# Splitting a kernel's weights by DMA: a cast on the way in, a negative, and an adding transfer

## The chip, the cores and the metric

The kernel runs on one core of a Trainium2 chip. The core has a matrix engine (TensorE, PE in the profile), a vector engine (VectorE, DVE), a scalar engine (ScalarE, ACT), a general engine (GpSimd, POOL) and a queue engine (SyncE, SP) that issues most transfers. Sixteen DMA engines, shared by all queues, move data between DRAM and the on-chip memory. The metric is the device time of one execution in microseconds, with the median of several runs; lower is better.

## The reference

One inference step of a two-layer recurrent decoder, in float32, for a prompt of 512 tokens and 8 single-token samples that share the weights (520 columns in all, width 1024). Cut to what matters here:

```
h  -> u = rmsnorm(h) @ w_in                     # layer 0: 1024 -> 5648
      a_out = RG-LRU(conv(a_x)) * silu(a_gate)
      b_out = groupnorm(SSD(conv(x, B, C), dt) * silu(z)) * w
h += concat(a_out, b_out) @ w_out               # 2048 -> 1024
h += sigmoid(h @ w_gate0) * (p0 @ w_proj0)      # 1024 -> 1024, 256 -> 1024

h  -> q, f, v, g = split(rmsnorm(h) @ w_in1)    # layer 1: 1024 -> 8192
      o = HGRN2(q, f, v) with 16 heads of 128
h += (rmsnorm_head(o) * silu(g)) @ w_out1       # 2048 -> 1024
h += sigmoid(h @ w_gate1) * (p1 @ w_proj1)
y  = rmsnorm(h)
```

The results are `y`, the recurrent states and the convolution buffers. Nearly all of the arithmetic is in the dense products with the weights, some 70 MB of float32.

## The kernel before

**Products.** Features lie on partitions, tokens along the free axis. Each dense product is made from float32r parts, a format of TensorE with fewer bits than float32: a weight tile w is split into `hi`, which is w cast to float32r, and `lo`, which is w − hi, and the activations are split likewise into xh and xl. A tile of 128 output features then takes, for each block of 128 input features, the products hi·xh, hi·xl and lo·xh, each over two halves of 260 columns (`project_both`, lines 682 to 701). A *unit* of weights is 128 × 1024 numbers, 512 KB; a full tile of outputs uses one unit in 8 × 6 = 48 matrix products. Two pairs of PSUM banks (`mmps`, line 560) take the outputs in turn, and ACT and DVE empty them.

**Weights.** `section` (line 609) cuts the matrices into units and puts neighbours into groups of one or two. `load_group` (line 619) loads a group of up to 1 MB from SP's queue into one of two raw buffers. `split_unit` (line 627) makes the parts: `hi` by a copy that casts, on ACT or DVE, whichever the plan finds free, and `lo` by a subtraction on DVE (POOL in two places at the start). Each part has two buffers, so a cast waits for the products of two units before. The sections come in the order in which they are used: `ax` (the RG-LRU input), the embedding's `proj0`, then `xbc` (12 units), `z`, `ag`, `z1`, `out0a`, `out0b`, `pg0`, `proj1`, and for layer 1 per pair of heads `f`, `v`, `q`, `g` with two units each, the output projection `o3`, `o5`, `o7`, `o8` with four units each, and `pg1`, the last gate.

**Order.** The program doesn't run in the order in which it is written. Every instruction is recorded with a place (`prio`) in the stream of dense products, which moves by 0.668 us for each block of six products (line 699). `side` shifts places earlier or later: loads by `LOAD_AHEAD` = 11.54 us, splits by `SPLIT_AHEAD` = 1.67 us. `Plan.order` (line 348) then lets an estimated clock run: an engine that comes free takes, of the instructions whose operands are there by that estimate, the one with the earliest place; instructions that the dense stream waits for are moved 38.78 us ahead. For a transfer it counts 1.0 us of POOL or 0.46 us of SP, 0.65 us until it starts, its bytes over 360 GB/s on one bus, and 1.0 us until it has landed (lines 466 to 472). The result is a fixed order for each engine; on the chip, semaphores make each instruction wait for its operands, and what is behind a waiting instruction on its engine waits with it.

**Around the dense stream.** In layer 0, ACT, DVE and POOL do the convolutions, the RG-LRU recurrence and the SSD scan. POOL computes the logarithm for `dt` in a row of small steps (`log1p_of`, line 920, called for `dt_project`, line 1168), prepares the sample columns and masks the decay matrices. In layer 1 each pair of heads has a chain of decay, products within chunks (A), key transposes (kt), states (kv) and outputs (o), whose matrix products PE takes between the dense ones, and POOL only takes a power of a few numbers per head.

**The last gate.** `layer1_end` (line 1973) goes over the tokens in two halves, each with all 8 units of `pg1`. Units 0 and 1 use the ordinary buffers; units 2 to 7 go to tiles of their own (`keep_acy`, `keep_z`, `keep_bx`) and stay for the second half. `pl1`, the embedding term of 2 MB, is loaded with one transfer 20 us ahead.

Nearly every instruction is issued at line 510, so the profile's groups are told apart by the names of tiles: `wraw` is a raw buffer, `whi` and `wlo` are the parts; a name such as `q` or `o` on PE is the output of that product.

Of the kernel before, what the change touches and what calls it, by code (L numbers as in the profile page):

```python
# [42 lines left out]
# how far ahead of a unit its weights are split and loaded, in us of the main stream  # L43
SPLIT_AHEAD, LOAD_AHEAD = 1.67, 11.54
# how far ahead of the main stream goes what it waits for, in us
MARGIN = 38.78
# an engine waits for an instruction that is more urgent by URGENT us, up to this part of the time of the one at hand
# [32 lines left out]
def _mm(n, a, k):  # L80
    out, m = k["out"] if "out" in k else a[0], k["lhsT"].shape[-1]
    if m < 128 and out.off >= 32 * ROW:
        # beside the one before it, in other columns of the array
        return 65 if k["rhs"].dtype == F32R else 125
    return max(n, 256) if k["rhs"].dtype == F32R else 4 * max(n, m)
# [17 lines left out]
class Buf:  # L103
    """A tile that is allocated when its first instruction is issued."""
# [7 lines left out]
class View:  # L112
    """A view of a Buf; offset and strides are in elements, a partition is ROW apart."""
# [86 lines left out]
class Op:  # L200
    """One instruction, in a form for each engine that may take it, or a few matrix products that stay together."""
# [8 lines left out]
class Plan:  # L210
    """Instructions are collected first and then put in an order: with an estimate of what each of them costs, an
    engine that comes free takes the instruction of the earliest place in the program whose operands are there."""
# [6 lines left out]
    # -- collecting --  # L219
# [23 lines left out]
    def side(self, start=0.0, rate=0.0, pinned=False):  # L243
        """Instructions whose place is moved, by a start and by their own time so far; pinned: for good."""
# [5 lines left out]
    @contextmanager  # L250
    def together(self, *views):
        """Instructions that wait until all of some operands are written."""
        self.gate = self.barrier([o for v in views for box, o, w in v.buf.acc if w and _meet(box, v.box())])
        yield
        self.gate = None

    @contextmanager
    def block(self, main=False):
        """Matrix products that stay together."""
# [66 lines left out]
    # -- ordering --  # L326
    def hold_banks(self):
        """A PSUM bank is taken only when what its readers wait for otherwise is already on its way."""
# [7 lines left out]
    def urgency(self):  # L336
        """What an instruction of the main stream waits for is put ahead of it."""
# [10 lines left out]
    def order(self):  # L348
# [44 lines left out]
        def pick(e, t):  # L393
            """The instruction for engine e at time t, or when there may be one."""
# [7 lines left out]
            while av:  # L402
# [13 lines left out]
                if func and table not in IN_SET[func]:  # L416
                    # another table: first what the loaded one can do, for a while
# [14 lines left out]
            if got:  # L432
                heapq.heappush(av, got)
                hold = {"dve": HOLD_DVE, "act": HOLD_ACT, "pool": HOLD_POOL}.get(e)
                if hold:
                    # rather wait a little for one that is more urgent than be in its way
# [8 lines left out]
        while left:  # L445
# [27 lines left out]
            else:  # L473
                if e == "pe":
                    # the clock is halved after a window with too few columns
# [17 lines left out]
    # -- issuing --  # L493
# [27 lines left out]
# the place of the side work: its start after the instructions it follows, and its pace  # L521
# [9 lines left out]
def hybrid_decode_step_kernel(ctx: ExitStack, tc: tile.TileContext, I, O, mode="both"):  # L531
# [31 lines left out]
    def grab(name):  # L563
        """One of four PSUM banks for the side work; it is given back by its last reader."""
# [26 lines left out]
    def copy(out, in_):  # L591
        """A copy on either engine."""
        plans[-1].record(("act", "copy", (out, in_), {}), ("dve", "tensor_copy", (out, in_), {}))

    def scaled(out, in_, s):
        """in_ times a column, on either engine."""
# [10 lines left out]
    groups, units, sec = [], [], {}  # L607

    def section(name, ap, k0, kk, c0, ncols, uc, per=2):
        sec[name] = len(units)  # L610
        for c in range(c0, c0 + ncols, per * uc):
            w = min(per * uc, c0 + ncols - c)
            groups.append((ap, k0, kk, c, w))
            for s in range(0, w, uc):
                units.append((len(groups) - 1, s, uc, kk))
# [3 lines left out]
    def load_group(g):  # L619
        ap, k0, kk, c, w = groups[g]  # L620
        r = new("wp", [128, 2048], "raw", f"wraw{g}", 2)
        v = r[:, :kk * w].rearrange("p (k c) -> p k c", k=kk)
        with side(*((plans[-1].shift, 0.0, True) if plans[-1].pinned else (-LOAD_AHEAD,))):
            sp.dma_start(out=v, in_=ap[k0 * 128:(k0 + kk) * 128, c:c + w].rearrange("(k p) c -> p k c", p=128))
        raw_of[g] = v

    def split_unit(u, hi=None, lo=None, eng=dve):
        g, s, uc, kk = units[u]
        if g not in raw_of:
            load_group(g)  # L630
        v = raw_of[g][:, :, s:s + uc]
        if hi is None:
            hi = new("wp", [128, 1024], "whi", f"whi{u}", 2, F32R)
            lo = new("wp", [128, 1024], "wlo", f"wlo{u}", 2, F32R)
        hv = hi[:, :kk * uc].rearrange("p (k c) -> p k c", k=kk)
        lv = lo[:, :kk * uc].rearrange("p (k c) -> p k c", k=kk)
        with side(*((plans[-1].shift, 0.0, True) if plans[-1].pinned else (-SPLIT_AHEAD,))):
            copy(hv, v)
            tt(lv, v, hv.bitcast(F32), SUB, eng)
# [5 lines left out]
    section("ax", w_in0, 0, 8, 0, 256, 128, 1)  # L645
    section("ax2", w_in0, 0, 8, 256, 768, 128)
    section("proj0", I["ple_proj"][0], 0, 2, 0, 512, 256, 1)
# [1456 lines left out]
```

## Time and profile before

| | |
|---|---|
| Median of 3 runs | 1074.88 us (1073.48 to 1077.2) |
| Profiled execution, first to last instruction | 1075.0 us |
| Mean granted clock of TensorE | 0.991 |
| Read from DRAM, written to DRAM | 111.71 MB, 25.44 MB |
| Weight loads of 1 MB on SP's queue | 32 + 15 + 8 + 8 + 8 + 1 |

The profile gives no other time for the profiled execution than its span, which is the time from its first to its last instruction. All views below are of this one execution. A group of instructions is shown by line, engine, operation, output and inputs with shapes and count, then the total busy time and the mean in ns of one, then the idle time of the engine just before them with what ended it. In a view of stretches each row has a stretch, its length, and the busy time and instruction count of each engine in it. The chain that ended last is followed back from the last instruction, each step to what released it.

### The profile page before, as it was taken

What the parts mean: (1) busy time and instruction counts of PE and PEld (TensorE: products, weight loads), DVE (VectorE), ACT (ScalarE), POOL (GpSimd) and SP (SyncE); (2) the same over time, 40 slices, a digit from 0 to 9 for tenths busy, and PEclk for the clock granted to TensorE, in tenths of its full rate; (3) what the DMA queues carried; (4) which work ended last, traced back from release to release, by engine and by line L of the source; (5) the groups of instructions that cost most, each with busy time, mean ns of one, the idle gap of its engine ahead of it and who ended that gap; (6) DMA issues with size and microseconds to landing.
All of it is one profiled execution on the core that took longest, in us unless ns stands there. A gap on an engine that the chain in (4) does not pass through costs nothing.

```text
span 1075.0 us, 21235 instructions
## 1 busy us (share of the span) xinstructions
PE 1044.0 (97%) x8595; PEld 1023.0 (95%) x8595; DVE 778.2 (72%) x1521; ACT 509.1 (47%) x1196; POOL 144.6 (13%) x247
## 2 busy tenths in 40 slices
PE   9899989999999999999999999999999999999995
PEld 8899988899999999999999999999999999999995
DVE  6879988999997546774858576675765757667753
ACT  6476648636464212353445545333463344642453
POOL 3755475200000000100000000000000000000000
PEclk9899999999999999999999999999999999999998
DMA  8603226444686233563433433253342433335311
GB/s 275 244 21 99 80 51 206 147 142 140 200 249 210 79 115 131 162 208 88 135 108 115 128 102 111 90 155 91 115 124 87 143 98 112 97 89 199 119 40 44
DMA packets 130466, 138.43 MB, mean 129 GB/s; under 512 B 13704, under 2 KB 111128, under 8 KB 130344
## 3 DMA queue, kind: packets, MB, share of 16 engines
q1 hardware_dynamic: 130136, 136.93, 41.0%
q8 instruction: 69, 1.13, 0.4%
q14 instruction: 37, 0.30, 0.1%
q0 software_dynamic: 224, 0.06, 0.0%
HBM read 111.71 MB, written 25.44 MB: 128 GB/s over the span
## 4 chain that ended last, share of the span: by engine, by line
PE 84%; POOL 5%; DVE 4%; DMA 3%; ACT 2%; issue 1%; POOLq 0%; ACTq 0%; DVEq 0%
PE o L510 11%; PE g L510 10%; PE f L510 9%; PE v L510 9%; PE q L510 9%; PE pg L510 7%; PE ag L510 4%; PE ob L510 4%; PE z L510 4%; PE oa L510 3%; PE ax L510 3%; PE xbc L510 1%; POOL csm L510 1%; PE A L510 1%; PE kv L510 1%
## 5 line engine op out<-in xcount | busy, mean ns | idle before, releaser
L510 DVE TENSOR_TENSOR wlo<-wraw,whi 128x1024 fp32r<-128x1024 f32 (+1 forms) x143 | 173.4, 1213 | 3.2 <-ACT whi L510 1.8
L510 ACT CAST whi<-wraw 128x1024 fp32r<-128x1024 f32 (+1 forms) x63 | 65.2, 1036 | 126.3 <-PE q L510 41.2
L510 POOL TENSOR_TENSOR at__1873<-at__1873,nhalf 128x4 f32<-128x4 f32 (+1 forms) x24 | 20.8, 866 | 501.1 <-DVE at__1873 L510 501.1
L510 DVE CAST whi<-wraw 128x1024 fp32r<-128x1024 f32 x80 | 55.3, 692 | 36.7 <-PE v L510 11.9
L510 PE MATMUL g<-xh,whi 128*128 128x260 f32 x256 | 55.8, 299 | 0.0
L510 PE MATMUL q<-xh,whi 128*128 128x260 f32 x256 | 53.2, 289 | 0.0
L510 PE MATMUL o<-oh,whi 128*128 128x260 f32 x256 | 52.6, 286 | 0.0
L510 PE MATMUL v<-xh,whi 128*128 128x260 f32 x256 | 52.1, 285 | 0.0
L510 PE MATMUL v<-xh,wlo 128*128 128x260 f32 x256 | 51.5, 283 | 0.0
L510 PE MATMUL g<-xl,whi 128*128 128x260 f32 x256 | 51.5, 283 | 0.0
L510 PE MATMUL o<-oh,wlo 128*128 128x260 f32 x256 | 51.5, 283 | 0.0
L510 PE MATMUL g<-xh,wlo 128*128 128x260 f32 x256 | 51.5, 283 | 0.0
L510 PE MATMUL o<-ol,whi 128*128 128x260 f32 x256 | 51.4, 282 | 0.0
L510 PE MATMUL q<-xl,whi 128*128 128x260 f32 x256 | 51.4, 282 | 0.0
L510 PE MATMUL v<-xl,whi 128*128 128x260 f32 x256 | 51.4, 282 | 0.0
L510 PE MATMUL q<-xh,wlo 128*128 128x260 f32 x256 | 51.4, 282 | 0.0
L510 PE MATMUL f<-xh,whi 128*128 128x260 f32 x240 | 50.6, 292 | 0.0
L510 PE MATMUL f<-xl,whi 128*128 128x260 f32 x240 | 48.2, 282 | 0.0
L510 PE MATMUL f<-xh,wlo 128*128 128x260 f32 x240 | 48.2, 282 | 0.0
L510 DVE SCALAR_TENSOR_TENSOR l1a<-q,lbt,l1a 128x260 f32<-128x260 f32 (+1 forms) x32 | 14.0, 479 | 44.1 <-PE q L510 44.0
L510 DVE SCALAR_TENSOR_TENSOR l1c<-l1d,l1c 128x128 f32<-128x128 f32 x128 | 40.9, 345 | 0.6 <-ACT l1c L510 0.6
L510 PEld LDWEIGHTS o<-oh,whi 128*128 128x128 f32 x256 | 39.3, 189 | 0.9 <-issue 0.8
(507 smaller groups left out, 3362.2 us busy)
## 6 DMA issues: line engine op xcount, KB each, us to landing
wraw<-in_c_w_in_dram SPq DMA_DIRECT2D x32, 1024.0 KB
wraw<-in_ab_w_in_dram SPq DMA_DIRECT2D x15, 1024.0 KB
wraw<-in_ab_w_out_dram SPq DMA_DIRECT2D x8, 1024.0 KB
wraw<-in_ple_gate_dram SPq DMA_DIRECT2D x8, 1024.0 KB
l1c<-in_state_c_dram SPq DMA_DIRECT2D x16, 512.0 KB
out_dram<-l1c SPq DMA_DIRECT2D x16, 512.0 KB
wraw<-in_c_w_out_dram SPq DMA_DIRECT2D x8, 1024.0 KB
pl<-pl_d SPq DMA_DIRECT2D x2, 2080.0 KB
```

The costliest lines, as they stand in the source:

```text
L510: getattr(f, name)(*a, **k)
```

## The change

All units from section `xbc` on are split in another way. There is no raw tile and no subtraction:

1. POOL issues a transfer from DRAM into `hi`, which casts to float32r on the way.
2. ACT or DVE writes `lo` = −hi (`scaled` with −1.0, on whichever engine the plan finds free).
3. POOL issues a second transfer of the same weights from DRAM into `lo`, with addition: lo = −hi + w.

Step 1 is placed 17.0 us ahead of the unit's products, steps 2 and 3 9.0 us ahead. Sections `ax`, `proj0` and `proj0b` keep the old way, with one unit per load instead of groups. The two raw, two hi and two lo buffers become eight equal buffers of one unit, which raw, hi and lo tiles share in turn. In the last gate, the transfers of units 2 to 7 wait until the `lo` part of the unit ahead of the gate is written, and `pl1` is loaded in eight pieces at places from −12 us on, 2.67 us apart. The other lines of the diff only remove comments.

```diff
-SPLIT_AHEAD, LOAD_AHEAD = 1.67, 11.54
+SPLIT_AHEAD, LOAD_AHEAD, HI_AHEAD, LO_AHEAD = 1.67, 11.54, 17.0, 9.0
...
-    def load_group(g):
-        ap, k0, kk, c, w = groups[g]
-        r = new("wp", [128, 2048], "raw", f"wraw{g}", 2)
...
+    def wtile(name, u, dt=F32R):
+        _, kk, uc = units[u]
+        return new("wp", [128, 1024], "wb", f"{name}{u}", 8, dt)[:, :kk * uc].rearrange("p (k c) -> p k c", k=kk)
+
+    def ahead(us):
+        return side(*((plans[-1].shift, 0.0, True) if plans[-1].pinned else (-us,)))
+
+    def load_raw(u):
+        raw_of[u] = wtile("wraw", u, F32)
+        with ahead(LOAD_AHEAD):
+            sp.dma_start(out=raw_of[u], in_=units[u][0])
...
     def split_unit(u, hi=None, lo=None, eng=dve):
...
+        ap, kk, uc = units[u]
+        early = u < sec["xbc"]
+        if early and u not in raw_of:
+            load_raw(u)
...
+        if early:
+            with ahead(SPLIT_AHEAD):
+                copy(hv, raw_of[u])
+                tt(lv, raw_of[u], hv.bitcast(F32), SUB, eng)
+        else:
+            with ahead(HI_AHEAD):
+                pool.dma_start(out=hv, in_=ap)
+            with ahead(LO_AHEAD):
+                scaled(lv, hv.bitcast(F32), -1.0)
+                pool.dma_start(out=lv, in_=ap, accum_op=ADD)
...
     def layer1_end(pl1, ytk, ytk4, keep, pre):
-        with side(-20.0):
-            sp.dma_start(out=pl1, in_=pl_d[1].rearrange("k p n -> p k n"))
+        for j in range(8):
+            with side(-12.0 + 2.67 * j):
+                sp.dma_start(out=pl1[:, j], in_=pl_d[1][j])
...
-            with side((j - 2) * 2.67, pinned=True):
+            with side((j - 2) * 2.67, pinned=True), plans[-1].together(split_of[u0 - 1][1]):
                 split_unit(u0 + j, t[:, o:o + 1024], t[:, o + 1024:o + 2048])
```

More of the change, by code (lines that the diff above doesn't have):

```diff
@@ L604, in ltile, with section @@
         return new("lay", shape, name, name, dt=dt)
-    groups, units, sec = [], [], {}
-    def section(name, ap, k0, kk, c0, ncols, uc, per=2):
+    units, sec = [], {}
+    def section(name, ap, k0, kk, c0, ncols, uc):
         sec[name] = len(units)
[L611 to L615, printed above, removed]
@@ L617, in hybrid_decode_step_kernel @@
-    raw_of, split_of = {}, {}
-    def load_group(g):
-        ap, k0, kk, c, w = groups[g]
-        r = new("wp", [128, 2048], "raw", f"wraw{g}", 2)
[L622 to L625, printed above, removed]
-    def split_unit(u, hi=None, lo=None, eng=dve):
[L628 to L639, printed above, removed]
+        for c in range(c0, c0 + ncols, uc):
+            units.append((ap[k0 * 128:(k0 + kk) * 128, c:c + uc].rearrange("(k p) c -> p k c", p=128), kk, uc))
@@ new lines, in hybrid_decode_step_kernel @@
+    raw_of, split_of = {}, {}
+    def wtile(name, u, dt=F32R):
[7 more added lines that the diff above has]
+            sp.dma_start(out=raw_of[u], in_=units[u][0])
+    def split_unit(u, hi=None, lo=None, eng=dve):
+        ap, kk, uc = units[u]
+        early = u < sec["xbc"]
+        if early and u not in raw_of:
+            load_raw(u)
+        hv, lv = (wtile(nm, u) if t is None else t[:, :kk * uc].rearrange("p (k c) -> p k c", k=kk)
+                  for nm, t in (("whi", hi), ("wlo", lo)))
+        if early:
[8 more added lines that the diff above has]
+                pool.dma_start(out=lv, in_=ap, accum_op=ADD)
@@ L644, in hybrid_decode_step_kernel @@
     XBC = [8, 10, 0, 1, 2, 3, 4, 5, 6, 7, 9, 11]
-    section("ax", w_in0, 0, 8, 0, 256, 128, 1)
+    section("ax", w_in0, 0, 8, 0, 256, 128)
     section("ax2", w_in0, 0, 8, 256, 768, 128)
-    section("proj0", I["ple_proj"][0], 0, 2, 0, 512, 256, 1)
-    section("proj0b", I["ple_proj"][0], 0, 2, 512, 512, 512, 1)
+    section("proj0", I["ple_proj"][0], 0, 2, 0, 512, 256)
+    section("proj0b", I["ple_proj"][0], 0, 2, 512, 512, 512)
     section("xbc", w_in0, 0, 8, 3072 + 1024, 128, 128)
@@ L738, in hybrid_decode_step_kernel @@
         with side(-69.0, pinned=True):
-            load_group(units[sec["proj0"] + i][0])
+            load_raw(sec["proj0"] + i)
         with side(-67.0 + i * W1, pinned=True):
@@ L744, in hybrid_decode_step_kernel @@
             if i == 1:
-                load_group(units[sec["proj0b"]][0])
+                load_raw(sec["proj0b"])
             if i == 2:
```

## The prediction

> **What bounds the kernel now.** I read the page's span and busy rows first, then the chain that ended last, then the stages, then what TensorE (PE) itself waited for.
>
> ```profile
> span 1075.0 us, 21235 instructions
> ...
> PE 1044.0 (97%) x8595; PEld 1023.0 (95%) x8595; DVE 778.2 (72%) x1521; ACT 509.1 (47%) x1196; POOL 144.6 (13%) x247
> ...
> PE 84%; POOL 5%; DVE 4%; DMA 3%; ACT 2%; issue 1%; POOLq 0%; ACTq 0%; DVEq 0%
> ```
>
> PE is busy for 1044.0 of 1075.0 us, so only 31 us are open to anything that doesn't shorten PE's own work. The change leaves every matrix product as it is. The stages say where the 31 us lie (columns: stretch, its length, then busy time and count of PE, PEld, DVE, ACT, POOL, then granted clock, DMA share, GB/s):
>
> ```profile
> 0.00:97.00 97.00, 89.09 (x663) 85.67 (x664) 74.25 (x141) 59.96 (x109) 51.57 (x103) 0.96 0.51 166
> ...
> 118.00:205.00 87.00, 80.23 (x655) 75.96 (x656) 76.98 (x124) 58.59 (x130) 45.42 (x77) 0.98 0.35 115
> 205.00:304.00 99.00, 98.71 (x825) 94.57 (x822) 93.59 (x183) 51.70 (x190) 2.74 (x3) 1.00 0.55 169
> 304.00:352.00 48.00, 47.14 (x391) 46.90 (x392) 39.99 (x67) 25.62 (x71) 3.56 (x2) 1.00 0.69 220
> 352.00:461.00 109.00, 106.83 (x887) 106.13 (x886) 64.50 (x93) 26.78 (x39) 3.87 (x10) 1.00 0.42 134
> 461.00:1009.00 548.00, 548.00 (x4567) 540.79 (x4567) 374.79 (x816) 245.04 (x574) 20.77 (x24) 1.00 0.39 117
> 1009.00:1064.00 55.00, 52.60 (x442) 52.04 (x440) 32.09 (x69) 29.56 (x67) 1.11 (x2) 1.00 0.17 58
> ```
>
> Layer 1 (461 to 1009) has no open time at all: PE 548.00 of 548.00 at full clock. Layer 0 from the x/B/C projections on (118 to 461) has 6.8 + 0.3 + 0.9 + 2.2 = 10.2 us, almost all before 205. What ended PE's waits in that part:
>
> ```profile
> PE acs L510 <- POOL dtt L510: 4.2, 1, 4.2
> PE pl L510 <- ACT plt L510: 2.2, 1, 2.2
> ...
> PE yd L510 <- DVE wsl L510: 1.8, 1, 1.8
> ...
> PE st L510 <- ACT bcs L510: 0.6, 1, 0.6
> ...
> PE oa L510 <- DVE aol L510: 0.4, 1, 0.4
> ```
>
> The largest is a wait on POOL, the engine to which the change gives work. ACT and DVE account for little, and DVE, at 72%, is not what sets the end.
>
> **The change part by part.** From section xbc on there are 142 weight units of 512 KB: 54 in layer 0 (12 xbc, 8 z, 8 ag, 16 output projection, 8 gate, 2 embedding), 80 in layer 1 (64 input, 16 output) and 8 for the last gate.
>
> *What it removes.*
>
> ```profile
> L510 DVE TENSOR_TENSOR wlo<-wraw,whi 128x1024 fp32r<-128x1024 f32 x141 | 172.0, 1220 | 3.2 <-ACT whi L510 1.8
> L510 ACT CAST whi<-wraw 128x1024 fp32r<-128x1024 f32 x61 | 64.0, 1049 | 122.9 <-PE q L510 41.2 <-PE ob L510 37.7 <-PE o L510 33.2
> ...
> L510 DVE CAST whi<-wraw 128x1024 fp32r<-128x1024 f32 x80 | 55.3, 692 | 36.7 <-PE v L510 11.9 <-PE f L510 11.8 <-PE pg L510 6.7
> ```
>
> 142 subtractions of 1.220 us go: 173 us of DVE. The casts go too, but a negative of the same shape takes the place of each, on ACT (1.049) or DVE (0.692): nothing. In layer 1 PE waits for neither engine, so 80 of the subtractions are worth nothing. In layer 0 the DVE- and ACT-caused waits that a freer DVE can shorten are yd 1.8, st 0.6 and oa 0.4: **−2.8 us**. The pl wait of 2.2 is not counted, as its ACT copy waited for a store to DRAM:
>
> ```profile
> 459.48 0.59 ACT L510 COPY plt<-pl 128x520 f32<-128x520 f32 x1 [3.38 <-DMA pl_d<-plt]
> ```
>
> *What it adds on POOL.* 284 transfers leave SP's queue (71 of 1 MB there before; SP's own time was free) for POOL's. The trace has small POOL transfers only:
>
> ```profile
> L510 POOL DMA_DIRECT2D prow<-in_a_lam_dram x1: 511/511/511, 3.9 to 3.9; - x1
> L510 POOL DMA_DIRECT2D prow<-in_b_conv_w_dram x1: 532/532/532, 4.4 to 4.4; - x1
> ...
> DMA to landing us min/median/max: 4.0/5.5/6.2
> ```
>
> The first moves 8 rows of 128 numbers, the second 48: 21 ns for 40 rows, 0.5 ns a row. A unit is 1024 such rows, so I estimate 0.51 + 1016 × 0.0005 = 1.04 us per transfer. Were the whole 532 ns the rows' price it would be 11 us, but 8 rows cost nearly as much as 48, which excludes that. In layer 1 POOL gets 160 × 1.04 = 166 us beside its 20.8 of 548: free. In layer 0 it matters between 118 and 205:
>
> ```profile
> 131.12 0.71 POOL L510 TENSOR_TENSOR htmp<-dtt,htmp 128x80 f32<-128x80 f32 x1 [0.58 <-DVE htmp L510]
> ...
> 138.94 1.05 POOL L510 TENSOR_TENSOR htmp<-htmp 128x80 f32<-128x80 f32 x1
> ...
> 145.34 0.35 POOL L510 TENSOR_TENSOR htmp<-htmp 128x80 f32<-128x80 f32 x1
> 145.78 0.43 POOL L510 TENSOR_SCALAR htmp<-htmp 128x80 f32<-128x80 f32 x1
> 146.29 0.35 POOL L510 TENSOR_TENSOR dtt<-dtt,htmp 128x80 f32<-128x80 f32 x1
> ```
>
> This is the logarithm for dt, 15.5 us of POOL nearly without a break, and acs waits for its end. PE takes 5.76 us per unit:
>
> ```profile
> 543.97 5.76 PE q L510 x48
> ```
>
> In 15.5 us it uses 2.7 units, so 5.4 transfers belong in that stretch: 5.4 × 1.04 = 5.6 us more, between 0 (all are put before or after it; eight buffers hold 4 units) and 11 (each slowed twofold, as below). I take **+5.6**.
>
> The rows just quoted show one instruction at 1.05 us while DVE was busy and at 0.35 once DVE stood still (143 to 148). So POOL may pay up to threefold beside DVE, and I carry that as a rival. The Trainium skill ("SBUF — State Buffer", § SBUF: two separate sides) has descriptors from POOL starve while a DVE copy or cast holds a shared port, about 620 ns becoming 3100; by it a transfer would cost five times 1.04, an estimate from that page, and POOL would be the bound everywhere. The threefold is the trace's nearest sign of it, and the trace has no large POOL transfer to show more.
>
> *What it adds on the DMA engines.*
>
> ```profile
> q1 hardware_dynamic: 130136, 136.93, 41.0%
> ```
>
> 136.93 MB took 41.0% of 1075 us, 311 GB/s with all 16 engines at work, so a unit costs 1.7 us of them. The raw load cost that once; now the cast costs it, and the adding transfer again: between 1.7 (the same bytes) and 5.1 (a read of the weights, a read and a write of the old contents, each at the full price). I take 2.55, as a copy is a read and a write and this adds one read. Per unit 4.25. Layer 1: 80 × 4.25 = 340, plus what isn't weights (0.39 × 548 − 80 × 1.7 = 78): 418 of 548. Layer 0 from 118: 54 × 4.25 = 230, plus 0.35 × 87 + 0.55 × 99 + 0.69 × 48 + 0.42 × 109 − 54 × 1.7 = 72: 302 of 343. Both fit; the engines are no bound, but busy enough for transfers to be late.
>
> *What it adds as a wait.* The chain of a unit is cast in, negative, adding transfer. With the landing row above (taken in a stretch with DMA share 0.51) a cast lands 4.0 to 6.2 + 1.7 = 5.7 to 7.9 us after its start, the negative takes 0.7 to 1.05, the addition 6.5 to 8.8: 12.9 to 17.7 in all. A buffer pair comes free when the unit four back is done, 3 × 5.76 = 17.3 us ahead: enough but for the top end. But the planner (lines 466 to 472) counts 1.0 + 0.65 + 1.46 + 1.0 = 4.1 us for that landing and puts the negative in ACT's or DVE's order accordingly. The engine then stands 1.6 to 3.8 us with what is queued behind it; POOL likewise behind the adding transfer. PE's real pace of 5.76 against the plan's 8 × 0.668 = 5.34 gives 0.3 of it back. Behind the negative are evacuations of main products, which have a unit of slack (two PSUM pairs), and steps of a head's chain (decay, A, kt, kv, o), whose products PE has at fixed places in its order and has none. ACT is idle 303 and DVE 173 of the 548 us, which hides most. The cost lies between 0 and 80 × 1.3 = 104 us; I take one stall of 1 us for each of 8 pairs of heads, near the lower end since PE now waits there for nothing: **+8**.
>
> *The end.* The kept units 2 to 7 of the last gate may not load before the last addition of the unit ahead is there.
>
> ```profile
> 1009.11 0.28 PE L510 MATMUL pg<-xh,whi 128*128 128x256 f32 x1
> ```
>
> ```profile
> 1013.22 8.06 DMA wraw<-in_ple_gate_dram
> ...
> 1025.24 2.50 PE pg L510 x21
> ```
>
> Today the last load lands at 1021.3, ahead of its use. With the change, the last output unit starts at 1009.1 − 5.8 = 1003.3, its buffers come free at 1003.3 − 17.3 = 986, so its addition lands at about 986 + 15 (the middle of the chain) = 1001, and the six follow at 4.25 us each: 1001 + 25.5 + 6 for the last landing = 1032.5. PE needs unit 7 at 1009.1 + 7 × 24 × 0.119 = 1029 (the pace is the 21 in 2.50 us). That is 3.5 late, up to 19 at the dear price, 0 or less at the cheap one; loading pl in eight pieces moves the same bytes. I take **+4**.
>
> *Sum.* 1075.0 − 2.8 + 5.6 + 8 + 4 = 1089.8, say **1090 us**, made against the profiled span of 1075.0; the median of the runs is 1074.88, so nothing has to be added. The start (before 97) keeps the old way, with single units instead of pairs: nothing.
>
> **The rivals.**
> - **It gains.** Transfers land as early as the plan thinks (4.1 + 0.3 us), so no stall and no late end, and the planner uses the freer DVE to move main products into the 4.2 us before acs: 1075 − 2.8 − 4.2 = 1068. Against it: the landing row's lowest is 4.0 for 24 KB and less. For it: those landed in a stretch with the DMA engines half busy. The Trainium skill ("DMA: Bandwidth & Descriptors", § Anatomy of one DMA — SWDGE path) gives about 2.0 us plus bytes over 436 GB/s; by it a unit would land in 3.2 us, an estimate from that page, and my +8 would fall away. No row here has such a landing.
> - **Nothing moves.** The stalls stay hidden in idle ACT and DVE, layer 0 gains what POOL loses: 1072 to 1078.
> - **POOL becomes the bound**, by DVE holding it up. At the threefold, 3.1 us: layer 1 has 160 × 3.1 + 20.8 = 517 of 548, fits; layer 0 has 108 × 3.1 + 55.6 (its own four stages) = 390 against 343: +47, in place of the 5.6. 1075 − 2.8 + 47 + 8 + 4 = 1131. It decides from (343 − 55.6) / 108 = 2.7 us per transfer. Against it: the change itself takes 30% of DVE's work in layer 0 away.
> - **The adding transfer bounds.** At 5.1, layer 1 needs 80 × 6.8 + 78 = 622 of 548, +74; layer 0 54 × 6.8 + 72 = 439 of 343, +96; the end +19: 1264. It decides in layer 0 from 5.0 per unit, in layer 1 from 5.9.
>
> **How the numbers follow.** Stalls as summed (1079 to 1115): 0.34. Gain (1060 to 1071): 0.27. Nothing: 0.17. POOL bound: 0.12. Adding transfer bound: 0.10. A measurement of this kernel tells about 0.3% (3.2 us) from no change: faster 0.27, same 0.17, slower 0.56. The range 1062 to 1200 leaves out the dearest transfers and the best of the gain; cases of both signs are in it, and the likeliest one's own range is 1079 to 1115.
>
> **What would show it.** DVE's busy time falls by about 170 us; ACT's stays within 70. POOL's transfers show about 1.0 us each: above 2.7 I am wrong on POOL. DMA share in layer 1 near 0.76: above 0.95, wrong on the addition. In layer 1 PE's row falls from 548.00 of 548 to some 8 us of idle, with ACT or DVE waiting for a DMA into whi: if PE stays solid, my stall term is wrong. The wait of acs on POOL grows from 4.2. A wait for a keep tile appears after 1009. If the span is under 1070, the landing was early and the planner found a better order in layer 0.

## The result and the profile after

| | before | after |
|---|---|---|
| Median | 1074.76 us of 4 runs (1073.48 to 1077.2) | 1304.52 us of 4 runs (1303.03 to 1323.83) |
| Ratio, 95% interval | | 1.2131 [1.2108, 1.2154] |
| Profiled execution, span | 1075.0 us | 1301.3 us |
| Mean granted clock of TensorE | 0.991 | 0.937 |

The change costs 21%. One of the four runs after fell into a slower state (1323.83 us at a granted clock of 0.928); the ratio and its interval are those of the other three (1303.03 to 1305.78). The profile of the changed kernel, its page: span, busy time and instructions of each engine, DMA share in 40 slices (tenths), the queues, the share of each engine in the chain that ended last.

```profile
span 1301.3 us, 21612 instructions
...
PE 1111.5 (85%) x8595; PEld 1072.6 (82%) x8595; DVE 611.2 (47%) x1397; ACT 521.4 (40%) x1168; POOL 479.0 (37%) x531
...
DMA  8459997899999999988997979799897998779981
...
q0 software_dynamic: 276128, 148.98, 75.3%
q1 hardware_dynamic: 62312, 62.48, 16.0%
...
PE 13%; DMA 12%; issue 12%; POOL 5%; ACT 2%; DVE 0%; POOLq 0%; ACTq 0%
```

PE runs the same 8595 instructions, but it is busy 85% of the time instead of 97%, and the chain is no longer PE's (84% before). The chain could be followed back only to 706 us, so its shares add up to 44% of the span and speak for the second half; there transfers and unexplained waits (`issue`) each weigh about as much as PE. POOL's queue (q0) had 0.06 MB before and now fills 75.3% of the sixteen DMA engines' time. With SP's queue that makes 91.3%, where it was 41.0%. DVE lost 167 us of work and nothing came of it.

The same kernel by stages (columns as before; the bounds are the first products of xbc, z, the output projection, its second half, layer 1 and the last gate, with the gate of layer 0 in the fourth row):

```profile
94.00:197.00 103.00, 83.99 (x655) 80.86 (x654) 69.52 (x124) 52.97 (x97) 68.86 (x108) 0.92 1.01 165
197.00:337.00 140.00, 123.47 (x1003) 114.68 (x1001) 96.26 (x202) 67.80 (x224) 50.24 (x53) 0.99 1.01 183
337.00:407.00 70.00, 52.65 (x395) 51.58 (x396) 32.74 (x65) 22.96 (x63) 21.11 (x18) 0.88 1.12 216
407.00:537.00 130.00, 113.38 (x889) 111.14 (x888) 41.68 (x69) 33.35 (x48) 51.15 (x50) 0.95 1.13 189
537.00:1226.00 689.00, 594.65 (x4566) 576.66 (x4565) 274.13 (x732) 250.61 (x566) 211.27 (x183) 0.93 0.90 154
1226.00:1301.00 75.00, 56.01 (x444) 54.16 (x442) 28.57 (x69) 33.02 (x70) 15.91 (x14) 0.91 0.65 113
```

Layer 1 took 548 us and takes 689, so it holds 141 of the 226 us; layer 0 from xbc on gives 78, the last gate 10, and the start gains 3. The DMA share is 1.01 to 1.13 through all of layer 0 (a share above 1 means that the times counted for packets overlap) and 0.90 in layer 1. PE's busy time in layer 1 has grown too, from 548.0 to 594.7 us for the same products, with a mean granted clock of 0.93 in place of 1.00.

The waits of the changed kernel (total, times, longest), its transfers (KB each, median us from issue to landing), and three instructions of its timeline (start, duration, in brackets the idle time ahead and what ended it):

```profile
POOL wlo L510 <- ACT wlo L510: 294.6, 57, 14.0
ACT wlo L510 <- DMA whi<-in_c_w_in_dram: 250.3, 39, 13.0
...
PE kv L510 <- ACT l1b L510: 29.3, 9, 5.4
...
PE q L510 <- DMA wlo<-in_c_w_in_dram: 17.2, 9, 3.8
...
PE bn0t L510 <- POOL rbn L510: 10.7, 1, 10.7
...
PE ah L510 <- POOL ahs L510: 10.2, 1, 10.2
```

```profile
whi<-in_c_w_in_dram POOLq DMA_DIRECT2D x63, 512.0 KB, 9.0
wlo<-in_c_w_in_dram POOLq DMA_DIRECT2D x63, 512.0 KB, 7.4
```

```profile
605.16 1.06 ACT L510 ACTIVATE wlo<-whi 128x1024 fp32r<-128x1024 f32 x1 [8.37 <-DMA whi<-in_c_w_in_dram]
...
606.52 1.60 POOL L510 DMA_DIRECT2D wlo<-in_c_w_in_dram  x1 [8.23 <-ACT l1c L510]
607.46 1.59 POOL L510 DMA_DIRECT2D whi<-in_c_w_in_dram  x1
```

Here is how a late transfer reaches PE. A cast of the largest group lands 9.0 us after its issue, where the plan counts 4.1, and an addition 7.4 us after its own. ACT stands in front of the negative, 8.37 us in this one case, with everything behind it in its queue; POOL stands in front of the addition (8.23 us). Behind the negatives in ACT's order are steps of a head's chain (`l1b`), and PE waits 29.3 us for those, 1.7 times what it waits for the parts of the `q` weights themselves (17.2). Before, none of the four PE rows but `bn0t` (0.7 us) was among PE's ten largest waits.

So the profile offers two causes. **Theory A:** the DMA engines are full, because casting and adding transfers cost them more than plain ones. **Theory B:** the order is wrong, because it was cut for transfers that land after 4 us. The experiments take them apart. All of them are changes of the changed kernel, unless they say otherwise, and single runs unless a number of runs is given. Before ran at 1075 to 1079 us beside them, 4 us apart from one group of runs to the next, so differences of a few us decide nothing.

### The profile page after: what moved, and what is told of

Read it like the earlier page. It is cut to its first block, busy times and chain, and to the rows that moved or that the text cites. A ratio compares the mean times of both kernels' runs of the same rounds, so it can differ in the third digit from the quotient of the medians.

```text
span 1301.3 us, 21612 instructions
## 1 busy us (share of the span) xinstructions
PE 1111.5 (85%) x8595; PEld 1072.6 (82%) x8595; DVE 611.2 (47%) x1397; ACT 521.4 (40%) x1168; POOL 479.0 (37%) x531
## 3 DMA queue, kind: packets, MB, share of 16 engines
q0 software_dynamic: 276128, 148.98, 75.3%
q1 hardware_dynamic: 62312, 62.48, 16.0%
## 5 line engine op out<-in xcount | busy, mean ns | idle before, releaser
L510 ACT ACTIVATE wlo<-whi 128x1024 fp32r<-128x1024 f32 x115 | 121.7, 1059 | 482.9 <-DMA whi<-in_c_w_in_dram 250.3
L510 POOL DMA_DIRECT2D wlo<-in_c_w_in_dram x63 | 99.0, 1600 | 345.2 <-ACT wlo L510 135.2
L510 POOL DMA_DIRECT2D whi<-in_c_w_in_dram x63 | 79.9, 1398 | 19.3 <-PE f L510 8.8
L510 POOL DMA_DIRECT2D wlo<-in_ab_w_in_dram x28 | 44.1, 1576 | 85.0 <-ACT wlo L510 30.2
L510 PE MATMUL q<-xh,wlo 128*128 128x260 f32 x256 | 55.1, 298 | 17.3 <-DMA wlo<-in_c_w_in_dram 17.2
L510 PEld LDWEIGHTS q<-xh,wlo 128*128 128x128 f32 x256 | 41.9, 200 | 19.3 <-DMA wlo<-in_c_w_in_dram 19.3
L510 POOL DMA_DIRECT2D wlo<-in_ab_w_out_dram x16 | 25.6, 1661 | 82.2 <-ACT wlo L510 48.3
L510 PE MATMUL f<-xh,whi 128*128 128x260 f32 x240 | 55.1, 314 | 0.0
L510 PE MATMUL f<-xh,wlo 128*128 128x260 f32 x240 | 52.0, 301 | 3.0 <-DMA wlo<-in_c_w_in_dram 3.0
L510 PE MATMUL f<-xl,whi 128*128 128x260 f32 x240 | 52.3, 302 | 0.0
```

What stands on the lines that cost most here:

```text
L510: getattr(f, name)(*a, **k)
```

## Experiments: the price and the order

**The addition left out.**

```diff
-                pool.dma_start(out=lv, in_=ap, accum_op=ADD)
+                pool.dma_start(out=lv, in_=ap)
```

> The changed kernel, with the second transfer a plain cast that overwrites the negative (the low part of the weights is then the weights themselves). Same number of transfers, rows, waits and the same order. Theory A: the second transfer's rows fall from 65 to 42 ns, 5.4 us per unit: layer 1 is no longer bound (80 x 5.4 + 78 = 510 of 548 us), layer 0 nearly (54 x 5.4 + 72 = 364 of 343 us), 1100 to 1160 us. Theory B: the first transfer still lands far later than the 4.1 us planned and ACT still stands in front of it, 1220 us or more.

The second transfer then writes the weights over the negative, so this kernel leaves the low part of the weights out. Measured: 1100.34 us, at the low end of what A forecast and far from B's 1220. The flag doesn't enter the plan, so the order of all engines is the changed kernel's, instruction by instruction. From its page, and one row of the stretches view (layer 1):

```profile
PE 1048.6 (95%) x8595; PEld 1023.6 (93%) x8595; DVE 607.6 (55%) x1397; ACT 527.8 (48%) x1168; POOL 383.5 (35%) x531
...
q0 software_dynamic: 276128, 148.98, 71.7%
...
whi<-in_c_w_in_dram POOLq DMA_DIRECT2D x63, 512.0 KB, 5.7
```

```profile
470.60:1032.90 562.30, 551.27 (x4562) 541.96 (x4561) 273.75 (x731) 258.06 (x568) 160.43 (x185) 1.00 0.93 190
```

The same bytes in the same number of packets take 71.7% of 1098.5 us, which is 788 us of the engines' time, instead of 75.3% of 1301.3, which is 980. In this order, that the second transfer adds costs 192 us of the engines and 204 us of the time. The 204 are not theory A alone, though: with packets that take less time the casts also land after 5.7 us instead of 9.0, so the same order fits better, and POOL is busy for 383.5 us instead of 479.0.

**The plan told the price.**

```diff
-                bus = max(bus, clk[e] + 0.65) + max(op.size / 360e3, 0.02)
+                bus = max(bus, clk[e] + (1.6 if e == "pool" else 0.65)) + max(op.size / (160e3 if e == "pool" else 360e3), 0.02)
```

> The changed kernel, with the planner told what a POOL transfer really takes (start 1.6 us after the issue and 160 GB/s, in place of 0.65 us and 360 GB/s: 6.9 us to landing in place of 4.1). Only the order of instructions can change. Theory A (the DMA engines are the bound: the changed kernel's rows of 512 B take about 42 ns with the cast and 65 ns with the addition, so 64 rows per engine and unit of each are 6.9 us, more than PE's pace): no order helps, 1260 to 1310 us. Theory B (the order is wrong: negatives stand at the head of ACT's queue waiting for a cast that lands 5 us later than planned, and all behind them is late): below 1150 us.

Measured: 1222.43 us. It lies between the two forecasts. The transfers are the same, only the order is another, and 82 us come back: theory B has a share. But then the engines are full:

```profile
PE 1087.0 (89%) x8595; PEld 1054.9 (86%) x8595; DVE 618.3 (51%) x1395; ACT 531.7 (44%) x1172; POOL 476.6 (39%) x531
...
DMA  9438998999999999998999999999998999989961
...
q0 software_dynamic: 276128, 148.98, 80.7%
q1 hardware_dynamic: 62312, 62.48, 17.1%
```

**Each half of the change alone.** In the first run the cast stays with POOL, but the raw weights come by SP and DVE subtracts; in the second the cast is ACT's or DVE's, and the negative and the adding transfer stay. The last gate stays as changed in both. Both have two raw buffers and a ring of six for the parts (six buffers taken in turn), so a part can be written only two units ahead. The new branch of the first (shortened):

```diff
+        plain = not early and u < sec["pg1"]
...
+        elif plain:
+            with ahead(HI_AHEAD):
+                pool.dma_start(out=hv, in_=ap)
+            with ahead(LO_AHEAD):
                 tt(lv, raw_of[u], hv.bitcast(F32), SUB, eng)
```

> From xbc to the last gate only the cast is done by a POOL transfer; the weights are also loaded raw on SP's queue, and the subtraction is back on DVE (the last gate stays as changed). Per unit about 64 x 27 = 1.7 us raw and 2.7 us cast of the DMA engines. Theory A: 80 x 4.4 + 78 = 430 of 548 us and 54 x 4.4 + 72 = 310 of 343 us, no bound: 1080 to 1120 us. Theory B: DVE now stands in front of the late cast as ACT did: 1180 us or more.

> From xbc to the last gate the cast is done by ACT or DVE from a raw load on SP's queue; the negative and the adding transfer stay (the last gate stays as changed). Per unit 1.7 us raw and 4.2 us addition of the DMA engines. Theory A: 80 x 5.9 + 78 = 550 of 548 us and 54 x 5.9 + 72 = 391 of 343 us: at the bound, 1130 to 1180 us. Theory B: nothing but PE waits for the adding transfer, which has 11 us for its 7: 1080 to 1110 us.

Measured: 1149.62 us for the cast alone, 1211.04 for the addition alone (in that one ACT or DVE casts from the raw tile, then writes the negative). Both are outside both forecasts: the cast alone is 30 us above A's range, the addition alone 31. The addition is the dearer half, as A says. But the cast alone costs 73 us with the engines at 78%, more than A has room for. A further run gave the cast four `hi` buffers (three units ahead in place of two):

```diff
-        return new("wp", [128, 1024], "wb", f"{name}{u}", 6, dt)
+        return new("wp", [128, 1024], name, f"{name}{u}", 4 if name == "whi" else 2, dt)
```

> The casting transfer alone (no adding transfer: raw weights on SP's queue, subtraction on DVE), as in the run that did the cast alone, but with four hi buffers instead of a ring of six for both parts, so that a cast may be issued three units ahead instead of two. If that run's 73 us over the kernel before came of a lookahead too short for a landing of 5.5 us: 1075 to 1110. If they came of the cast as such (its rows, or POOL standing behind a buffer): 1140 or more.

Measured: 1110.73 us, just past the end of what lookahead was to give, but 39 of the 73 us are back with the same transfers. What a ring covers looks like a third cause, and the runs further down follow it.

**What makes a casting row dear.** First all units in the old split, with the rest of the change kept; then the same with the plain loads issued by POOL.

```diff
-        early = u < sec["xbc"]
+        early = True
```

```diff
-            sp.dma_start(out=raw_of[u], in_=units[u][0])
+            (pool if u >= sec["xbc"] else sp).dma_start(out=raw_of[u], in_=units[u][0])
```

> All units are split in the old way again (a plain transfer on SP's queue into a raw buffer, a cast, a subtraction), but the rest of the change stays: one unit per load instead of pairs, rings of four, the last gate's order, pl1 in eight pieces. Theory A (the rows of the casting and adding transfers fill the DMA engines) and theory B (negatives stand at the head of ACT's queue for a cast that lands later than the plan counts) both say that the loss goes away whole: 1070 to 1082. A third, that smaller loads, eight equal buffers or the later order of the last gate cost something by themselves: 1090 or more, with the loss where PE waits for a raw buffer or after 1009.

> As the run before it in this list, but the plain loads into the raw buffers are issued by POOL, without a cast. It measures what makes a casting row of 512 B dear (42 ns against 27 ns from SP). If the cast does, the rows fall to about 27 ns and the POOL queue's share is about 142 x 64 x 27 ns = 0.25 ms per engine, 23% of the span. If the queue that POOL fills does, they stay at about 42 ns, and the share is about 0.38 ms, 35%. Time in both cases 1070 to 1100, as the engines are far from full.

Measured: 1072.66 us (median of 10 runs), ratio 0.9976 [0.9961, 0.9991] to before, and 1080.79 us. Without the new split nothing of the loss is left; the 0.24% by which the first is better than before is too little to build on. So the single loads, the late gate and `pl1` in pieces are cleared. The eight buffers that raw, hi and lo share are not, as these two runs have a ring of four for the raw tiles and another of four for the parts. No other version of this study is faster than before. The queues of the two runs, the first with loads on SP and the second with loads on POOL:

```profile
q1 hardware_dynamic: 200264, 136.94, 44.5%
```

```profile
q0 software_dynamic: 20672, 74.52, 24.0%
q1 hardware_dynamic: 62312, 62.48, 19.4%
```

From these rows every price follows, as share × span over the number of units (142):

| transfer of one unit | worked out from | us of all 16 engines |
|---|---|---|
| plain, from SP | (44.5% × 1067.5 − 19.4% × 1079.0) / 142 | 1.87 |
| plain, from POOL | 24.0% × 1079.0 / 142 | 1.82 |
| casting | 71.7% × 1098.5 / 284 | 2.77 |
| casting + adding | 75.3% × 1301.3 / 142 | 6.90, so adding 4.13 |

POOL's queue as such is no dearer than SP's; the cast makes a transfer 1.5 times as dear and the addition 2.2 times. The runs with the cast alone and the addition alone (above), taken apart by these prices, give nearly the same: 2.83 for a cast, 4.20 for an addition. Spread over a unit's 1024 rows of 512 B, 64 on each engine, that is 29, 43 and 65 ns per row (the 16 units of an output projection in layer 1 have longer rows, so these are rough). Nor is it full engines that make the price: where every second unit alone is changed (below), with a share of 0.71 in layer 1, a changed unit costs 42.6% × 1176.9 / 71 = 7.1.

The expectation named one thing wrongly. It compared rows of 512 B, but POOL's plain loads went out in 20672 packets of 3.6 KB on average, where casting ones are cut into 512 B. So the same bytes on the same queue cost more when they are cast; whether by the conversion or by the small packets that come with it is not shown. SP's plain loads go in small packets too, 137952 of 540 B on average (200264 − 62312), at 1.87 us per unit; no run has small plain packets on POOL's queue.

**With both at once**, the plan told the price and no addition:

> Leaves the addition out (the second transfer writes the weights over the negative) and lets the plan count the real price of POOL's transfers (1.6 us until it starts, 160 GB/s). Theory A: engine time falls to about 0.99 ms, under PE's own, so that with the order put right little is left: 1072 to 1092. Theory B alone says the same as the run that only knows the price would have said, so that the addition's share is the difference to it, 1222 less this: 130 to 150 us. If the 25 us that are left without the addition are not of the order: 1095 to 1105 again.

Measured: 1169.55 us. Both theories missed. The order is that of the run that was told the price, instruction by instruction. In it the addition costs 53 us (1222.43 to 1169.55), where it cost 204 in the changed kernel's order, so the two causes don't simply add up. And without the addition this order is 69 us worse than the changed kernel's (1100.34). The plan now counts some 6.6 us of the bus per unit (two transfers of 512 KB at 160 GB/s), while two casting transfers take 5.5; that an order cut for transfers slower than the real ones loses like one cut for faster ones is a likely reason, but no run shows it.

**Only the landing corrected.**

```diff
-                fin = bus + 1.0
+                fin = bus + (5.0 if e == "pool" else 1.0)
```

> The changed kernel, but the plan counts 4 us more until a transfer of POOL has landed (8.1 in place of 4.1 for a unit), and the old price on the bus. Theory B: the negatives no longer stand ahead of their casts, so the 80 us that the whole price in the plan was worth come back: 1215 to 1240, and ACT's 250 us of waiting for casts fall by more than half. If those 80 us came of counting the price of the rows (a slower stream for the rest of the order), little comes back: 1270 to 1305. Theory A alone: no lower than 1190 in either case.

Measured: 1220.09 us, as B forecast. Four microseconds in the plan's landing give back 84 of the 230 by which the medians differ, as much as the whole price in the plan did, so a later landing is enough to explain that gain. ACT's waits for casts from `c_w_in`, in this kernel:

```profile
ACT wlo L510 <- DMA whi<-in_c_w_in_dram: 46.0, 9, 12.4
```

46.0 in place of 250.3 us. And here too the engines end full (queues 81.1% and 17.3%).

## Experiments: half the load, and what the buffers cover

If full engines are the bound, half the new transfers should be nearly free. Here every second unit is split the changed way and the others by subtraction, with four buffers for the changed parts (three units ahead, as in the changed kernel), two for the others and two raw.

```diff
-        early = u < sec["xbc"]
+        early = u < sec["xbc"] or u % 2 == 0
...
-        return new("wp", [128, 1024], "wb", f"{name}{u}", 8, dt)
+        return new("wp", [128, 1024], "wb" if u % 2 else "we", f"{name}{u}", 4 if u % 2 else 2, dt)
```

> Every second unit from xbc on is split in the changed way, the others by subtraction; rings of four (changed units), two and two raw (the others), so that a casting transfer may be issued as far ahead as in the changed kernel. By the queue rows so far a plain unit costs 1.87 us of the DMA engines and a changed one 6.9, so two units need 8.8 us against 11.5 of PE: the engines are no bound. Theory A: the loss goes almost whole, 1070 to 1090, and the landing of a cast falls from 9.0 to below 6 us. Theory B (each negative that waits for a late cast costs, 71 of them here): half of the 80 us that the order was worth, 1110 or more.

Measured: 1178.59 us, 100 over before. Layer 1 in this run:

```profile
502.60:1099.10 596.50, 560.99 (x4560) 550.09 (x4561) 333.89 (x815) 243.42 (x531) 117.54 (x103) 0.98 0.71 142
```

The DMA share is 0.71, and the casts from `c_w_in` land after 5.8 us, below the 6 that A named as its sign. Theory A's forecast of the time fails all the same: the engines have room on average, and most of the loss of half a change is still there. Two more runs on the same kernel, the plan told the later landing, and the addition left out:

> Every second unit in the changed way, as before, and the plan counts 4 us more until a transfer of POOL has landed. The half cost 100 us though its mean load on the DMA engines (0.7 in layer 1) leaves them room. If that loss is the order's (negatives at the head of ACT's and DVE's queues for casts that land later than planned): 1075 to 1100, and what is left of the whole change with the same plan (1220) is the engines'. If it comes of the buffers (rings of four and two) or of bursts at the engines, the plan can't mend it: 1150 or more.

> Every second unit in the changed way, order as in the first half run, but the addition is left out, so that the second transfer writes the weights themselves at the price of a cast (2.8 us of the engines in place of 4.2). If the adding rows are what delays things even at half the load: 1075 to 1105. If the order and the buffers cost it whatever the second transfer does: 1150 to 1180.

Measured: 1174.89 and 1141.46 us. Before ran at 1075.21 beside these two, 3.9 us below its time beside the first half run. Over before, the later landing leaves the loss at 99.7 us, where it gave back 84 in the full change, so B is not this loss either. Leaving out the addition, in the same order, brings it to 66: about a third of the loss, between the two forecasts, so the adding transfers are a part of it and not the whole. The chain of waits of the run with the later landing, in order of time (start, duration, what), says why:

```profile
620.13 1.64 PE f L510 x12
621.77 0.06 issue
621.83 8.66 DMA whi<-in_c_w_in_dram
630.49 5.67 issue
636.16 0.02 POOLq L510
636.18 9.77 DMA wlo<-in_c_w_in_dram
645.95 0.04 issue
645.99 6.97 PE q L510 x56
```

The products of `f` free a buffer at 621.8; the cast into it lands at 630.5, DVE writes the negative from 634.7 on, the addition is issued at 636.2, it lands at 645.9, and only then PE goes on: 24 us, where three units of PE's pace are 17.3. (Why the negative began 4 us after the landing, the view doesn't tell.) **Theory C:** the buffers don't cover a unit's chain. The last three runs test it by depth, with the casts placed earlier to use it. The first is a control with one raw buffer, which makes room for one `hi` buffer more in the second (a cast up to five units ahead). The third is the full change with the later landing in the plan, the eight buffers cut into five for `hi` and three for `lo` in place of a shared ring, casts placed 22 us ahead and negatives 10.

```diff
-        return new("wp", [128, 1024], name if u % 2 else "we", f"{name}{u}", 2 if u % 2 and name == "whi" else 2, dt)
+        return new("wp", [128, 1024], name if u % 2 else "we", f"{name}{u}", 3 if u % 2 and name == "whi" else 2, dt)
...
-SPLIT_AHEAD, LOAD_AHEAD, HI_AHEAD, LO_AHEAD = 1.67, 11.54, 17.0, 9.0
+SPLIT_AHEAD, LOAD_AHEAD, HI_AHEAD, LO_AHEAD = 1.67, 11.54, 24.0, 9.0
```

> Every second unit in the changed way, the plan as in the changed kernel, one raw buffer instead of two (to make room in the next run): the control for the next run, with a casting transfer at most three units ahead of its products (17.3 us at PE's pace). Layer 1 took 596.5 us in the first half run against 547.4 before: about the same here, 590 to 610.

> As the run before it, with one hi buffer more for the changed units, so that a casting transfer may be issued five units ahead (28.8 us; its place is 24 us ahead in place of 17). In the half runs the chain of waits goes from the products that free a buffer through the cast (8.7 us), the wait for the negative (5 to 6) and the addition (9.8 to 11.8) to the products: 24 to 27 us against 17.3. Theory C, that the buffers don't cover the chain of a unit: layer 1 falls from about 596 to 550 to 570. If bursts at the DMA engines or the order at ACT cost it: 585 or more.

> The changed kernel with the plan that counts 4 us more, and its eight buffers cut into five for hi and three for lo, so that a casting transfer may be issued four units ahead (its place 22 us ahead in place of 17, that of the negative 10 in place of 9). Against 1220 with the shared ring of eight. Theory A: the DMA engines are full there (98% of the span), so nothing is gained: 1205 to 1235. Theory C: the chain is covered better, 1190 or less.

Measured: 1201.69 and 1149.27 us, so one buffer, with the earlier place that uses it, is worth 52 us, 25.8 of them in layer 1 (610.5 to 584.7, first product of `f` to that of the last gate). The forecast for C was 550 to 570, that of its rivals 585 or more: buffers that are too few cost time, but by this run they aren't even half of layer 1's loss. What PE waits for most in the deeper kernel is now the other half of the units, the plain ones with their single raw buffer, whose load took 12.80 us in this piece of its chain:

```profile
640.58 12.80 DMA wraw<-in_c_w_in_dram
653.38 0.02 issue
653.41 1.05 ACT whi L510
654.46 0.04 issue
654.51 1.23 PE q L510 x4
```

So some 37 us of the half's loss in layer 1 are not settled between the single raw buffer and plain loads that queue behind POOL's transfers. That the raw buffer has a share is likely: the control, with one raw buffer, took 14 us more in layer 1 than the first half run with two (610.5 against 596.5). But its rings were cut otherwise as well, so no run parts these two.

The full change with five and three: 1198.05 us, against 1220.09 with the shared ring; 1205 to 1235 was forecast by A, 1190 or less by C, and it fell between.

```profile
q0 software_dynamic: 276128, 148.98, 83.0%
q1 hardware_dynamic: 62312, 62.48, 17.7%
```

```profile
495.40:1123.00 627.60, 567.64 (x4562) 556.68 (x4561) 300.17 (x780) 231.56 (x523) 220.81 (x184) 0.95 1.02 170
```

The engines are full from the first product of `xbc` to the last gate: the share is 1.02 in layer 1, and 1.18 in the 401.2 us of layer 0 before it. By the changed kernel's own rows, the transfers need 75.3 + 16.0 + 0.4 = 91.7% of 1301.3 us, which is 1193 us of all engines, and the best order and buffers found reach 1198. That the two are so near is partly luck, and 1193 is no hard floor: the queues of this last run add up to 101.2% of 1196.3 us, 1211, more than its span, as the times counted for packets overlap, while the start and the last gate, 94 and 73 us, have shares of only 0.55 and 0.61.

**What the 226 us are, then.** About 106 (1304.5 to 1198) are late transfers: 84 of them go when the plan counts the landing, 22 more when the casts get deeper buffers. About 120 are left where the engines are full, with some 1193 us of transfers where PE's own work is 1044; these I put down to the price of the transfers. That is argued and not measured by itself: no order tried here got below 1198 with these transfers, and only leaving out the addition did, but what the addition costs hung on the order (204 us in one, 53 in another), and deeper buffers than five and three were not tried.

## Why the prediction was wrong, step by step

The direction was right (slower had 0.56), and the size was wrong by a factor of 15: +15 forecast, +226 measured.

**The step that failed** is the price under "What it adds on the DMA engines": 1.7 + 2.55 = 4.25 us per unit, and with it "Both fit; the engines are no bound". The unit costs 2.77 + 4.13 = 6.90. Both halves were too cheap. For the cast I took the plain price, as it moves the same bytes; for the addition I counted bytes, one read more. On these engines a cast took 1.5 times and an addition 2.2 times the plain price for the same bytes. With 6.90 the same sum gives 80 × 6.9 + 78 = 630 us for layer 1, and 627.6 was measured where the engines are full. The bound of 5.1 for the addition held (4.13); there was no bound above 1.7 for the cast, and there ought to have been one, as the trace of before had no casting transfer.

**A second step failed with it**: the stalls, +8 forecast, "near the lower end since PE now waits there for nothing". They measured about 106 of the 226 us (below).

**The rival "The adding transfer bounds"** had 0.10 and was half of the mechanism. Its conditions fit the runs ("It decides in layer 0 from 5.0 per unit, in layer 1 from 5.9"): at 6.9 the engines are full in both layers (shares 1.18 and 1.02 in the best run). Its 1264 was for 6.8 us per unit, near the 6.90 measured by luck, as its cast was 1.07 too cheap and its addition 0.97 too dear. It lies between the best run, 1198, and the 1301 to which late transfers raise it; layer 0 paid 36 us by the engines in the best run (365.2 before to 401.2, first product of xbc to that of layer 1), not 96. It was put at 0.10 because 6.8 was read as the end of a range and 4.25 as its middle; nothing in the trace spoke for the middle.

| Term | Forecast | Measured |
|---|---|---|
| DVE's relief in layer 0 | −2.8 | none: DVE fell by 167 us, as said, but PE's wait for `wsl` grew from 1.8 to 4.2 |
| POOL in the logarithm's stretch | +5.6 | PE's waits for POOL there 4.4 to 10.2: +5.8, near the forecast by luck, as it was for `ahs` and not for `dtt`; another 10.0 at `rbn`, not foreseen |
| Length of one transfer on POOL | 1.04 | casting 1.40, adding 1.60 (`c_w_in`), overlapping; casting 0.89 with the addition left out |
| Engines | 0 | about +120 |
| Stalls | +8, bounds 0 to 104 | about +106, just past the far end |
| End | +4, up to 19 | +9.6 (65.9 to 75.5) |

The rows overlap: engines and stalls make up the 226 us, and the waits for POOL and the end lie within them.

*The stalls.* The chain was right: cast late, negative at the head of ACT's queue, head steps behind it, PE. The size followed from a landing of 5.7 to 7.9 us; it was 9.0 for the largest group, and 5.7 with the addition left out. "enough but for the top end" was said of buffers that cover 17.3 us against a chain of 12.9 to 17.7; the chain followed in the half run took 24. That "ACT is idle 303 and DVE 173 of the 548 us, which hides most" doesn't help in a fixed order: idle time behind a wait can't be used.

*POOL.* The point of decision was 2.7 us per transfer. The means are 1.40 for a cast and 1.60 for an addition, and POOL is busy for 37% of the span, so it did not become the bound; of the 284 transfers only two, into tiles of the last gate, were longer than 2.7 (3.09 and 3.11 us). The Trainium skill ("SBUF — State Buffer", § SBUF: two separate sides) has POOL's descriptors starve beside DVE; the five-fold price worked out of it as an estimate, 5.2 us, is reached by none of them.

*The gain.* A landing as early as the plan counts (4.1 us) is found for some groups of the kernels without additions (3.9 us at the lowest median), and for none of the changed kernel, where the lowest is 6.2. The Trainium skill's price ("DMA: Bandwidth & Descriptors", § Anatomy of one DMA — SWDGE path), 3.2 us for such a unit by an estimate from that page, is below the lowest median of a unit in every run with units on POOL's queue; the measurements decide.

*The signs.* "DMA share in layer 1 near 0.76: above 0.95, wrong on the addition": 0.90 in the changed kernel and 1.02 in the one whose order fits. In the changed kernel the sign was blurred by its own stalls; the queue's total, 91.3% of a longer span, was the clearer one. DVE's busy time and ACT's came as said. PE's idle time in layer 1, "some 8 us", was 94. `acs` no longer waited for POOL, and PE shows no wait for a keep tile: the last of them took 16.0 us to land and held ACT's negative, and behind it in ACT's order stood work that PE waited for.

## What to carry to other kernels

Price a transfer by what is done on the way, not by its bytes alone: a cast or an addition on the way took 1.5 and 2.2 times the engines' time of a plain load here, and the total over all queues must be held against the time of the engine that bounds. Where the trace has no such transfer, bound each of its steps from above, and let that bound weigh as much as the middle. When a load becomes a chain of transfers, a fixed order needs its true landing and the buffers must cover the whole chain at the bounding engine's pace: the two were worth 84 and 22 us here, taken in this order.

## What the hardware showed

- An adding transfer of 1024 rows lasted 1.56 to 1.60 us on POOL in every run, full engines or not (mean of those from `c_w_in`: 1582 ns in the half run, 1600 in the changed kernel). Without the addition the same transfer took 0.88 to 0.89. A cast took 0.89 without additions around it and 0.93 to 1.48 among them. These lengths overlap: the next transfer began about 0.9 us after an addition (0.94 in the pair at 606.52 us), so an addition doesn't hold POOL for its whole length.
- The granted clock of TensorE was by and large lower in kernels in which PE stood more: mean 0.992 at a span of 1067.5 us, 0.978 at 1109.0, 0.951 to 0.968 at 1147.5 to 1220.7, 0.937 at 1301.3. In the changed kernel that made PE's own work longer, 1111.5 us in place of 1044.0, so 67 of the 226 us show as busy time. Which of the two causes the other was not tried.
- Plain loads of rows of 512 B went out from POOL in packets of 3.6 KB on average, the same loads from SP in packets of 540 B, at nearly the same engine time (1.82 and 1.87 us per unit).
